# Gate and scale units of the adaLN in three slots of their own, and x loaded again behind gate B, in a two-layer trunk kernel

## The chip, the cores and the metric

The kernel runs on one core of one Trainium2 chip, in one launch. The metric is the device time of an execution in microseconds (us), median over runs. One further execution was taken by the hardware profiler; every row below is from it.

## What is computed

Two groups of tokens, 128 context tokens and 256 latent tokens, together 384, go through two layers of width 2048. Each layer modulates its input by shift and scale of an adaLN (a matrix-vector product of the conditioning with a weight of 2048 x 6144), multiplies it by one wide input projection, runs two branches, and adds a gated output projection to x:

```
shift, scale, gate = split(silu(cond) @ w_mod + b_mod, 3)
h    = rms_norm(x, g) * (1 + scale) + shift
proj = h @ w_in
# layer 0
a = ga * sigmoid(gb); a = depthwise_conv(a, 31 taps) + conv_b
a = silu(layer_norm(a, ln_g, ln_b)) * silu(gate_a)          # branch A
b = attention(rms_norm(q), rms_norm(k), v) * silu(gate_b)   # branch B
x = x + gate * (concat(a, b) @ w_out)
# layer 1: windowed attention with a sink, beside a short gated convolution; then a final rms_norm
```

## The kernel before, in words

Everything is in float32. A product of two matrices is made of three fp32r products: each operand is split into a high and a low part (`hi`, `lo`), and `hi*hi + hi*lo + lo*hi` is summed in PSUM. The activations stand transposed, 16 blocks k of 128 features by 384 tokens, as `hhi` and `hlo`. Weights come by SyncE's DMA queue (SP) in pieces of 512 KB into six buffers `raw` (L106); ScalarE (ACT) casts `whi` (L283), VectorE (DVE) takes the difference `wlo` (L284), and TensorE (PE) multiplies (L382). `proj_feat` makes 256 output features from two units; a unit is two such pieces and 48 products, the first over k 0 to 7, the second over k 8 to 15.

The stretch that matters is layer 0 behind its q, k and v. In order of the source: four blocks of `gb` and `ga` (16 units), four of gate A (8 units), four of gate B (8 units, the loop that the change touches), then `out_proj`, whose first unit needs k 0 to 7 of `mix`, that is branch A. Counting units from the first `gb` one, gate A begins at unit 16, gate B at 24, the output projection at 32. Beside the products run:

- the adaLN by matrix-vector products (`gemv_block`): a unit is 1 MB of `mod_w` and four products with 32 rows (L139). 28 of them wait in `gemv_q`: eight for the bias of q, 16 for layer 0's gate, four for a quarter of layer 1's scale. After each projection unit `pump` adds `bg["rate"]` to what is due and starts as many. Without slots of their own they load two pieces into the same `raw` buffers as the weights;
- the rest of layer 1's adaLN by rows (`mod_rows`): GpSimd's DMA queue (POOL, L91) brings rows of the transposed weight, DVE multiplies and sums them (L207). The first two of these sets work in `lent`, the room of x (16 blocks of 384 in the place `bigA`), cut into three pieces of 2048: two for rows, one as junk;
- attention: norms and rotary on DVE and ACT, then for each of six pairs of token block and head group scores (`s_ps`, L505), softmax (L510 to L521), transposes (`pT_ps`, L526) and the output (`o_ps`, L530);
- the convolution, 30 taps a block on DVE (L702), and behind it the layer norm: sum (`lsum`), mean by PE (L755), `apad - mean` (L761), sum of squares `lvar` (L768), by PE a sum over features (`rsl`, L240), a reciprocal root on DVE (L229 to L234), three diagonals `diag` (L255), and a PE product that spreads them over the partitions (`rbl`, L256). ACT copies that to `rb` (L262), DVE multiplies by it (L771), ACT applies silu (L772), DVE multiplies into `mix` (L793), and `mix` is split into `hhi` and `hlo` (L283, L284).

Each engine works its instructions off in one order, which a scheduler fixed when the program was built, from priorities and from its own idea of times; instructions under `later(LATER)` come behind others that are ready. An instruction that waits holds all behind it on its engine or queue.

Of the kernel before, what the change touches and what calls it, by code (L numbers as in the profile page):

```python
# [10 lines left out]
F32 = mybir.dt.float32  # L11
# [8 lines left out]
P = 128  # L20
D = 2048
KC = D // P
T = 384
# [14 lines left out]
LATER = 4000  # L38
# [3 lines left out]
FILL = 3  # L42
R0 = 1.7
SCALE_AT = (9, 11)
RA = 1.2
RB = 1.1
GRID_W = 64
GROUPS = ((0, 0, SEQ), (1, SEQ, T))

# [2 lines left out]
def trunk(ctx: ExitStack, tc: tile.TileContext, d: dict, o: dict):  # L52
    nc = tc.nc
    const = ctx.enter_context(tc.tile_pool(name="const", bufs=1))
    big = ctx.enter_context(tc.tile_pool(name="big", bufs=1))
# [7 lines left out]
    def aux(name):  # L63
        return ps_aux.tile([P, 512], F32, tag="aux", name=name)
# [13 lines left out]
    def vcol(name, i):  # L78
        return vec(name)[:, i:i + 1]
# [10 lines left out]
    def side_load(dst, src):  # L90
        ins = nc.gpsimd.dma_start(dst, src).ins  # L91
        if order["hold"] is not None:
            tc.add_manual_dep(ins, order["hold"].name, SYNC, reason="side loads wait")
# [20 lines left out]
    ring = {"slots": [], "n": 0}  # L114
# [7 lines left out]
    def gemv_block(w, f0, nf, stat, done):  # L122
        nk = 2048 // nf
        st = {}

        def unit(u):
            if u == 0:
                st["ps"] = ps_gv.tile([P, 512], F32, tag="gv", name="gv")
            ps = st["ps"]
            slot = ring_slot()  # L130
            if slot is not None:
                raws = [load_w(w, nk * u, nk, f0, nf, slot.rearrange("p (k f) -> p k f", f=nf))]
            else:
                raws = [load_w(w, nk * u + nk // 2 * i, nk // 2, f0, nf) for i in range(2)]
            for i in range(nk):
                g = i % 4
                k = nk * u + i
                raw = raws[i * len(raws) // nk]
                nc.tensor.matmul(ps[32 * g:32 * g + 32, :nf], lhsT=stat(k), rhs=raw[:, i % raw.shape[1], :],  # L139
                                 start=(k < 4), stop=(k >= KC - 4))  # L140
            if nk * (u + 1) == KC:
                gs = tmp.tile([P, 512], F32, tag="gs", name="gs", bufs=1)
                nc.scalar.copy(gs[:, :nf], ps[:, :nf])
                done(gs, ps)
        return [lambda u=u: unit(u) for u in range(KC // nk)]

    def mod_tile(layer, part):
        m = const.tile([P, KC, 2], F32, name=f"mod{layer}{part}")
        mods[layer, part] = m
        return m  # L150

    def mod_finish(layer, part, sl, parts):
        n = sl.stop - sl.start
        b = vec(f"mod_b{layer}")[:, 16 * part:16 * part + 16]
        gn = vec(f"norm_g{layer}")
        dst = mods[layer, part][:, sl, :]
        if parts is not None:
            nc.vector.tensor_reduce(dst, parts, AX.X, ALU.add)
        bb = b[:, sl].unsqueeze(2).broadcast_to([P, n, 2])
        nc.vector.tensor_tensor(dst, dst, bb, ALU.add)  # L160
        if part == 1:
            gg = gn[:, sl].unsqueeze(2).broadcast_to([P, n, 2])
            nc.vector.scalar_tensor_tensor(dst, dst, 1.0, gg, ALU.add, ALU.mult)

    def mod_part(layer, part, widths=(512, 512, 512, 512), f0=0):
        if (layer, part) not in mods:
            mod_tile(layer, part)

        def consume(f0, nf, gs, pc):
            n = nf // P  # L170
            for i in range(n):
                nc.tensor.transpose(pc[:, i * P:(i + 1) * P], gs[:, i * P:(i + 1) * P], ident)  # L172
            sl = slice(f0 // P, (f0 + nf) // P)
            mod_finish(layer, part, sl, pc[:, :nf].rearrange("p (k g r) -> p k r g", g=4, r=32)[:, :, 0:2, :])
        units = []
        for nf in widths:
            units += gemv_block(d[f"mod_w{layer}"][4 * part + f0 // 512], f0 % 512, nf, lambda k: cst[:, 2 * k:2 * k + 32],
                                lambda gs, ps, f0=f0, nf=nf: consume(f0, nf, gs, ps))
            f0 += nf
        return units  # L180
# [55 lines left out]
    def rstd_cols(parts, mean, name, behind=None):  # L236
        ps = aux(name)
        for n, av in enumerate(parts):
            for t in range(NT):
                order["sum"] = nc.tensor.matmul(ps[:, t:t + 1], lhsT=av[:, t * P:(t + 1) * P], rhs=ones,  # L240
                                                start=(n == 0 and t == 0),
                                                stop=(n == len(parts) - 1 and t == NT - 1)).ins
                if behind is not None:
                    tc.add_manual_dep(order["sum"], behind.name, NOSYNC, reason="not before its place")
        rs = const.tile([P, NT], F32, name=name)
        nc.vector.tensor_scalar(rs, ps[:, :NT], 1.0 / mean, EPS, ALU.mult, ALU.add)
        (pow_half if behind is None else rsqrt)(rs)
        return rs

    def by_token(rs, name):  # L250
        pb = aux(name)
        dgs = tmp.tile([P, T], F32, tag="wk", name="diag", bufs=4)
        for t in range(NT):
            dg = dgs[:, t * P:(t + 1) * P]
            nc.vector.tensor_scalar(dg, ident, rs[:, t:t + 1], None, ALU.mult)  # L255
            nc.tensor.matmul(pb[:, t * P:(t + 1) * P], lhsT=ones.broadcast_to([P, P]), rhs=dg, start=True, stop=True)  # L256
        return pb[:, :T]

    def rstd_rows(rs, name):
        pb = by_token(rs, name)  # L260
        rb = tmp.tile([P, T], F32, tag="rb", name="rb", bufs=1)
        nc.scalar.copy(rb, pb)  # L262
        return rb

    x = {"T": big.tile([P, KC, T], F32, tag="bigA", name="xT")}
# [47 lines left out]
    gemv_q = []  # L313
# [19 lines left out]
    @contextmanager  # L333
    def later(n):
        p = tc.cur_priority
        tc.cur_priority = p + n
        try:
            yield
        finally:
            tc.cur_priority = p + 1  # L340

    def drain(lst):
        while lst:
            lst.pop(0)()
# [49 lines left out]
    def proj_feat(w, evac, units=(0, 1), n=T):  # L394
        pp = pair()
        for u in units:
            feat_unit(pp, w, u, n, u == units[0], u == units[1])
        for j in range(2):
            evac(j, pp[j])
# [274 lines left out]
    def add_bias(b, gs, pb):  # L674
        for g, ts in ((0, (0,)), (1, (1, 2))):
            nc.tensor.matmul(pb, lhsT=selb[:, g, :], rhs=gs, start=True, stop=True)  # L676
            for t in ts:
                x = nat[t][:, 4 * b:4 * b + 4, :]
                nc.vector.tensor_tensor(x, x, pb.rearrange("p (h c) -> p h c", h=4), ALU.add)
    bias_q = [f for b in range(2) for f in  # L680
              gemv_block(d["wq0"][0], 512 * b, 512, lambda k: sst[:, k, :], lambda gs, ps, b=b: add_bias(b, gs, ps))]
# [4 lines left out]
    def attention0():  # L686
        ss = head_norms(nat, mix)
        for t in range(NT):
            qkv_tile(0, t, kT, v, nat, mix, 8, ss)
        for t in range(NT):  # L690
            for kv in range(NKV):
                attend(0, t, kv, kT, v, mix, 8)
# [14 lines left out]
        return [lambda j=j: tap(j) for j in range(CONF)] + [done]  # L707

    bg["rate"] = R0
    gemv_q.extend(bias_q + mod_part(0, 2) + mod_part(1, 1, (512,)))  # L710
    lent = big.tile([P, KC * T], F32, tag="bigA", name="lent")
    slots = [lent[:, i * D:(i + 1) * D] for i in range(3)]
    shifts = [mod_rows(1, 0, j, slots) for j in range(2)]
    x["T"] = big.tile([P, KC, T], F32, tag="bigA", name="xT2")
    with later(LATER):
        side_load(x["T"], d["xT"])
    for fb in range(4):
        sgs = []

# [15 lines left out]
        if fb == 1:  # L735
            attention0()
            bg["rate"] = RA
            room = mix[:, :8, :].rearrange("p c t -> p (c t)")
# [31 lines left out]
    def ln_out(c):  # L770
        ln["out"] = nc.vector.tensor_tensor(apad[:, c, :T], apad[:, c, :T], ln["r"], ALU.mult).ins  # L771
        nc.scalar.activation(apad[:, c, :T], apad[:, c, :T], AF.Silu, scale=vcol("ln_g0", c), bias=vcol("ln_b0", c))  # L772
    bg["rate"] = RB

# [5 lines left out]
    for fb in range(4):  # L780
        proj_feat(w0[12 + fb], evb(2 * fb))
        if fb == 0:
            ln_mean()
            for c in range(8):
                ln_center(c)
        if fb == 1:
            ln["r"] = rstd_rows(rstd_cols([ln["v"]], CW, "rsl", order["product"]), "rbl")
            for c in range(8):
                ln_out(c)
            shifts.append(mod_rows(1, 0, 3, vring, ln["out"]))  # L790
            scales = [mod_rows(1, 1, j, vring, ln["out"]) for j in (1, 2, 3)]
# [239 lines left out]
```

## Time and profile before

| | us |
|---|---|
| median of 3 runs | 1292.69 (1292.29 to 1292.76) |
| the profiled execution | 1290.78 |
| its span, first to last instruction | 1289.0 |
| PE, DVE, ACT, POOL busy | 1255.9, 884.3, 556.0, 96.1 |
| HBM read | 253 MB, 199 GB/s over the span |

The span is what lies between the first and the last instruction; 1.8 us of the profiled execution lie around it. PE's busy time counts pipelined products, so a full share does not say that it ran at its best.

### The profile page before, as it was taken

To read this page: it belongs to the slowest core of one execution; us is meant where nothing else is said; L and a number is where in the kernel's file an instruction comes from. 1 tells how busy PE (TensorE), PEld (TensorE's weight loads), DVE (VectorE), ACT (ScalarE), POOL (GpSimd) and SP (SyncE) were. 2 spreads that over 40 slices of the span, in tenths; PEclk is the share of its full clock that TensorE was granted. 3 is DMA by queue.
4 is the path that set the end of the run, shared out by engine and by line. 5 is a ranking of instruction groups with operands and counts; after the bars stand their busy time and mean duration, and the time that the engine had idled before them with its cause. 6 is when DMAs were issued, how large, how long until landed. Compare 5 with 4: busy or idle time off the path is not lost.

```text
span 1289.0 us, 17822 instructions
## 1 busy us (share of the span) xinstructions
PE 1255.9 (97%) x6856; PEld 1115.2 (87%) x6856; DVE 884.3 (69%) x1507; ACT 556.0 (43%) x983; POOL 96.1 (7%) x137
## 2 busy tenths in 40 slices
PE   6999999999999999999999999999999999999997
PEld 3566576778888899999999988899999999999997
DVE  2244688999899967999977933354544599994443
ACT  3345422554455655543464632354444432343322
POOL 0211200000000000111100000000000011101110
PEclk9999999999999999999999999999999999999999
DMA  9989887868665334577743443433333588843322
GB/s 364 395 308 357 348 312 302 327 234 286 219 201 177 129 99 148 188 265 259 245 155 111 130 131 119 135 114 115 98 99 98 175 268 270 265 148 124 124 66 98
DMA packets 70500, 257.97 MB, mean 200 GB/s; under 512 B 7376, under 2 KB 11728, under 8 KB 65424
## 3 DMA queue, kind: packets, MB, share of 16 engines
q1 hardware_dynamic: 57616, 203.51, 46.6%
q0 software_dynamic: 12656, 53.23, 11.8%
q8 instruction: 53, 0.87, 0.3%
q14 instruction: 31, 0.25, 0.1%
q10 hardware_dynamic: 144, 0.10, 0.0%
HBM read 253.15 MB, written 3.67 MB: 199 GB/s over the span
## 4 chain that ended last, share of the span: by engine, by line
PE 95%; DVE 2%; DMA 1%; ACT 1%; issue 1%; SPq 0%; DVEq 0%; ACTq 0%
PE pf L382 67%; PE pt L361 10%; PE q L612 6%; PE gv L139 5%; PE s_ps L505 2%; PE o_ps L530 2%; PE pT_ps L526 1%; DMA raw<-in_mod_w 1%; DMA ring<-in_mod_w 1%; PE y_ps L915 1%; PE gv L172 0%; DVE wlo L284 0%; PE qT_ps L491 0%; DVE hlo L284 0%; PE gv L676 0%
## 5 line engine op out<-in xcount | busy, mean ns | idle before, releaser
L382 PE MATMUL pf<-hhi,whi 128*128 128x384 f32 (+1 forms) x1664 | 568.8, 342 | 3.7 <-ACT whi L283 3.6
L382 PE MATMUL pf<-hlo,whi 128*128 128x384 f32 (+1 forms) x1664 | 569.9, 343 | 0.0
L382 PE MATMUL pf<-hhi,wlo 128*128 128x384 f32 (+1 forms) x1664 | 562.1, 343 | 1.5 <-DVE wlo L284 1.5
L284 DVE TENSOR_TENSOR wlo<-raw,whi 128x1024 fp32r<-128x1024 f32 x256 | 312.9, 1223 | 281.9 <-ACT whi L283 271.1
L283 ACT CAST whi<-raw 128x1024 fp32r<-128x1024 f32 x256 | 268.3, 1050 | 461.8 <-PE pf L382 237.6
L382 PEld LDWEIGHTS pf<-hhi,whi 128*128 128x128 f32 x1664 | 313.3, 188 | 23.5 <-issue 11.9
L382 PEld LDWEIGHTS pf<-hhi,wlo 128*128 128x128 f32 x1664 | 312.9, 188 | 16.2 <-issue 6.7
L382 PEld LDWEIGHTS pf<-hlo,whi 128*128 128x128 f32 x1664 | 313.8, 189 | 5.3 <-issue 3.0
L207 DVE CUSTOM_DVE_ANT_0 area<-area,crow 128x1024 f32<-128x1024 f32 x128 | 151.5, 1218 | 5.3 <-PE o_ps L530 4.4
L702 DVE SCALAR_TENSOR_TENSOR cv<-apad,cw,cv 128x399 f32<-128x399 f32 x240 | 138.0, 627 | 0.1
L91 POOL DMA_DIRECT2D area<-in_modT x64 | 34.0, 531 | 575.8 <-DVE sm L207 233.7
L361 PE MATMUL pt<-wlo,hhi 128*128 128x512 f32 x192 | 75.8, 395 | 0.0
L361 PE MATMUL pt<-whi,hhi 128*128 128x512 f32 x192 | 75.4, 396 | 0.0
L361 PE MATMUL pt<-whi,hlo 128*128 128x512 f32 x192 | 74.1, 395 | 0.0
L276 POOL TENSOR_TENSOR sacc<-sacc,sqf 128x384 f32<-128x384 f32 x28 | 33.5, 1195 | 176.7 <-ACT sqf L275 175.9
L361 PEld LDWEIGHTS pt<-whi,hhi 128*128 128x128 f32 x192 | 36.0, 188 | 11.0 <-ACT hhi L308 1.7
L612 PE MATMUL q<-whi,hhi 128*128 128x512 f32 x96 | 41.1, 428 | 4.4 <-ACT hhi L295 4.4
L361 PEld LDWEIGHTS pt<-whi,hlo 128*128 128x128 f32 x192 | 35.9, 188 | 10.0 <-DVE wlo L284 1.7
L361 PEld LDWEIGHTS pt<-wlo,hhi 128*128 128x128 f32 x192 | 36.1, 188 | 9.1 <-issue 0.8
L139 PE MATMUL gv<-ring,cst 128*32 128x512 f32 (+1 forms) x288 | 35.6, 582 | 8.5 <-DMA ring<-in_mod_w 7.6
L513 ACT ACTIVATE pr<-s_ps,nm 128x384 f32<-128x384 f32 (+1 forms) x48 | 24.4, 508 | 43.6 <-DVE nm L512 34.4
L612 PE MATMUL q<-wlo,hhi 128*128 128x512 f32 x96 | 40.5, 422 | 0.0
(186 smaller groups left out, 995.0 us busy)
## 6 DMA issues: line engine op xcount, KB each, us to landing
raw<-in_wf SPq DMA_DIRECT2D x144, 512.0 KB, 4.1
ring<-in_mod_w SPq DMA_DIRECT2D x32, 1024.0 KB, 7.5
area<-in_modT POOLq DMA_DIRECT2D x64, 512.0 KB, 5.2
raw<-in_w_out SPq DMA_DIRECT2D x64, 512.0 KB, 4.0
raw<-in_mod_w SPq DMA_DIRECT2D x40, 512.0 KB, 5.5
raw<-in_wq SPq DMA_DIRECT2D x32, 512.0 KB, 8.8
raw<-in_wt SPq DMA_DIRECT2D x24, 512.0 KB, 3.6
lent<-in_modT POOLq DMA_DIRECT2D x8, 1024.0 KB, 8.2
```

The lines of the kernel that those rows point to most:

```text
L91: ins = nc.gpsimd.dma_start(dst, src).ins
L139: nc.tensor.matmul(ps[32 * g:32 * g + 32, :nf], lhsT=stat(k), rhs=raw[:, i % raw.shape[1], :], start=(k < 4), stop=(k >= KC - 4))
L207: ins = nc.vector.tensor_tensor_reduce(out=raw if g else junk, in0=raw, in1=crow[:, g, h * n:(h + 1) * n], scale=1.0, scalar=0.0, op0=ALU. ...
L276: eng.tensor_tensor(av, av, s, ALU.add)
L283: nc.scalar.copy(dst_hi, src)
L284: order["split"] = nc.vector.tensor_tensor(dst_lo, src, dst_hi.bitcast(F32), ALU.subtract).ins
L361: nc.tensor.matmul(pp[t], lhsT=x[:, k, tt], rhs=y[:, i, :], start=(k == 0 and n == 0), stop=(k == KC - 1 and n == 2))
L382: ins = nc.tensor.matmul(pp[j][:, :n], lhsT=x[:, i, fj], rhs=y[:, k, :n], start=(begin and k % 8 == 0 and m == 0), stop=(end and k % 8 == ...
L505: nc.tensor.matmul(ps, lhsT=mix[:, h0 + h, t * P:(t + 1) * P], rhs=kT[:, kv, c0:c0 + nk * P], start=True, stop=True)
L530: nc.tensor.matmul(po, lhsT=v[:, slots[j], kv * HD:(kv + 1) * HD], rhs=pT[:, j, :], start=(j == 0), stop=(j == nk - 1))
L612: nc.tensor.matmul(pq[b][t], lhsT=x[:, k, tt], rhs=y[:, 0, 512 * b:512 * b + 512], start=(k == 0 and n == 0), stop=(k == KC - 1 and n == 2))
L702: nc.vector.scalar_tensor_tensor(st["o"], apad[:, c, j:j + CVW], cw[:, c, j:j + 1], st["o"], ALU.mult, ALU.add)
```

## The change

The units of layer 0's gate and of layer 1's scale no longer load into `raw`: from the first of them on, `ring["slots"]` names the three pieces of `lent`, so each unit is one load of 1 MB into one of these. The bias units of q stay in `raw`. The room therefore is not given back to x before gate B; behind gate B's second block (units 24 to 27) the queue of units is emptied, the slots are taken away, and the 3 MB of x are loaded on POOL's queue, not under `later` any more. The rates of `pump` after attention is written and after the convolution fall from 1.2 and 1.1 to 0.9 and 0.8, which spreads the 20 units.

```
-RA = 1.2
-RB = 1.1
+RA = 0.9
+RB = 0.8
...
     bg["rate"] = R0
-    gemv_q.extend(bias_q + mod_part(0, 2) + mod_part(1, 1, (512,)))
     lent = big.tile([P, KC * T], F32, tag="bigA", name="lent")
     slots = [lent[:, i * D:(i + 1) * D] for i in range(3)]
     shifts = [mod_rows(1, 0, j, slots) for j in range(2)]
-    x["T"] = big.tile([P, KC, T], F32, tag="bigA", name="xT2")
-    with later(LATER):
-        side_load(x["T"], d["xT"])
+
+    def own_slots():
+        ring["slots"] = slots
+    gates0 = mod_part(0, 2) + mod_part(1, 1, (512,))
+    gates0[0] = lambda unit=gates0[0]: (own_slots(), unit())
+    gemv_q.extend(bias_q + gates0)
...
         if fb == 1:
+            drain(gemv_q)
+            ring["slots"] = []
+            x["T"] = big.tile([P, KC, T], F32, tag="bigA", name="xT2")
+            side_load(x["T"], d["xT"])
             ln["r"] = rstd_rows(rstd_cols([ln["v"]], CW, "rsl", order["product"]), "rbl")
```

The first place at which the built order differs is SP's queue, around unit 6 (`in_wf` are weights, `in_mod_w` adaLN units). Before:

```order
L98 DMA raw<-in_wf 128x1024 x2
L98 DMA raw<-in_mod_w 128x1024 x4
L98 DMA raw<-in_wf 128x1024 x2
L98 DMA raw<-in_mod_w 128x1024 x2
L98 DMA raw<-in_wf 128x1024 x2
```

and after:

```order
L98 DMA raw<-in_wf 128x1024 x2
L98 DMA lent<-in_mod_w 128x2048 x2
L98 DMA raw<-in_wf 128x1024 x2
L98 DMA lent<-in_mod_w 128x2048
L98 DMA raw<-in_wf 128x1024 x2
```

The same bytes stand in the same places; half as many loads, and none of them takes a buffer of the weights.

The second is PE around `rbl`, the last product of the layer norm. Before, it stands inside the sixth unit of gate B (`pf1_4207` is a pair of that gate):

```order
L382 MATMUL pf1_4207<-hlo_94,whi_4300 128x384
L382 MATMUL pf1_4207<-hhi_93,wlo_4301 128x384
L256 MATMUL rbl_4080<-diag_4081,ones_83 128x128 x3
L382 MATMUL pf1_4207<-hhi_93,whi_4300 128x384
L382 MATMUL pf1_4207<-hlo_94,whi_4300 128x384
```

and after, where `pf1_4275` is the last pair of gate B and `pf0_4443` the first of the output projection:

```order
L382 MATMUL pf1_4275<-hlo_94,whi_4368 128x384
L382 MATMUL pf1_4275<-hhi_93,wlo_4369 128x384
L256 MATMUL rbl_4020<-diag_4021,ones_83 128x128 x3
L382 MATMUL pf0_4443<-hhi_93,whi_4447 128x384
L382 MATMUL pf1_4444<-hhi_93,whi_4447 128x384
L382 MATMUL pf0_4443<-hlo_94,whi_4447 128x384
```

Before, 102 products of gate B stand between `rbl` and the output projection; after, none. The mean of the layer norm (L755) moved the same way, from behind 26.98 units to behind 29.25, the sum for `rsl` from 28.94 to 31.10, and `rbl` from 29.88 to 32.00.

The third is DVE between the multiplication by `rb` and the first `hlo` of the output projection. Before, behind the eight L771:

```order
L207 ISA area,sm_4106<-area,crow 128x1024
L207 ISA sm_4106 128x1
L284 TENSOR_TENSOR wlo<-raw,whi 128x1024
L565 TENSOR_TENSOR mix_1217<-mix_1217,sg 128x384
L793 TENSOR_TENSOR mix_1217<-mix_1217,apad 128x384 x5
L207 ISA area,sm_4106<-area,crow 128x1024
L207 ISA sm_4106 128x1
L207 ISA area,sm_4106<-area,crow 128x1024
L207 ISA sm_4106 128x1
L793 TENSOR_TENSOR mix_1217<-mix_1217,apad 128x384 x3
L284 TENSOR_TENSOR wlo<-raw,whi 128x1024
L284 TENSOR_TENSOR hlo<-mix_1217,hhi 128x384 x3
```

and after, where the line numbers stand two and six higher (L773 is L771, L799 is L793):

```order
L773 TENSOR_TENSOR apad<-apad,rb 128x384 x8
L565 TENSOR_TENSOR mix_1217<-mix_1217,sg 128x384
L207 ISA area,sm_4046<-area,crow 128x1024
L207 ISA sm_4046 128x1
L284 TENSOR_TENSOR hlo<-mix_1217,hhi 128x384 x3
L799 TENSOR_TENSOR mix_1217<-mix_1217,apad 128x384 x7
L207 ISA area,sm_4046<-area,crow 128x1024
L207 ISA sm_4046 128x1
L207 ISA area,sm_4046<-area,crow 128x1024
L207 ISA sm_4046 128x1
L799 TENSOR_TENSOR mix_1217<-mix_1217,apad 128x384
L284 TENSOR_TENSOR hlo<-mix_1217,hhi 128x384 x8
```

The work is the same, but after, the splits of branch B's blocks (the three `hlo`, and the first of the eight) come ahead of branch A's, whose k 0 is the second of the eight. Ahead of L773 there now stand one `wlo` of unit 33 and three L565.

## Rows read from the trace of the kernel before

**Rows 1.** Span and mean granted clock of the core.
```profile
core 0: 1289.0 us, clock 0.995
```
**Rows 2.** The page's chain that ended last, shares of the span by engine.
```profile
PE 95%; DVE 2%; DMA 1%; ACT 1%; issue 1%; SPq 0%; DVEq 0%; ACTq 0%
```
**Rows 3.** Busy time by stretches; columns in the first line.
```profile
core 0: us, PE busy (x) PEld busy (x) DVE busy (x) ACT busy (x) POOL busy (x), PEclk, DMA share, GB/s
210.00:230.00 20.00, 18.81 (x99) 13.77 (x98) 18.93 (x27) 6.86 (x18) 0.53 (x1) 1.00 0.79 301
230.00:250.00 20.00, 16.98 (x91) 12.67 (x90) 19.83 (x38) 14.45 (x56) 0.00 (x0) 1.00 0.98 383
...
270.00:290.00 20.00, 17.82 (x96) 11.79 (x95) 17.37 (x27) 12.12 (x28) 1.38 (x3) 0.91 0.79 270
...
450.00:470.00 20.00, 20.00 (x107) 18.63 (x106) 17.62 (x30) 11.83 (x22) 0.00 (x0) 1.00 0.28 87
470.00:490.00 20.00, 20.00 (x110) 18.16 (x109) 10.80 (x18) 11.66 (x20) 1.57 (x3) 1.00 0.52 175
```
**Rows 4.** Chain that ended last, in order of time: start us, us, what.
```profile
236.89 5.81 DMA raw<-in_mod_w
...
272.37 3.77 DMA raw<-in_mod_w
...
508.77 9.49 PE pf L382 x54
...
518.29 1.09 DVE area L207
...
531.92 132.24 PE pf L382 x752
```
**Rows 5.** Waits of SP's queue, 225 to 285 us: total us, times, longest.
```profile
SPq L98 <- PE gv L139: 33.3, 10, 9.2
```
**Rows 6.** DVE in order of time, last set of rows in `lent`: start, us.
```profile
222.88 2.29 DVE L207 CUSTOM_DVE_ANT_0 lent<-lent,crow 128x2048 f32<-128x2048 f32 x1
```
**Rows 7.** Loads: size, median us to landing.
```profile
xT<-in_xT POOLq DMA_DIRECT2D x1, 3072.0 KB, 13.1
```
**Rows 8.** PE in order of time at `rbl` and in the output projection's first unit.
```profile
507.94 0.83 PE L256 MATMUL rbl<-diag,ones 128*128 128x128 f32 x6
...
531.92 0.45 PE L382 MATMUL pf<-hhi,wlo 128*128 128x384 f32 x1 [0.34 <-DVE wlo L284]
```
**Rows 9.** DVE in order of time, layer norm to first split.
```profile
500.15 0.16 DVE L246 TENSOR_SCALAR rsl<-rsl 128x3 f32<-128x3 f32 x1 [2.10 <-PE rsl L240]
...
503.81 0.68 DVE L255 TENSOR_SCALAR diag<-ident,rsl 128x128 f32<-128x128 f32 x3
...
509.32 3.84 DVE L771 TENSOR_TENSOR apad<-apad,rb 128x384 f32<-128x384 f32 x8 [1.15 <-ACT rb L262]
513.08 1.22 DVE L207 CUSTOM_DVE_ANT_0 area<-area,crow 128x1024 f32<-128x1024 f32 x1
...
515.83 2.42 DVE L793 TENSOR_TENSOR mix<-mix,apad 128x384 f32<-128x384 f32 x5
...
521.87 1.22 DVE L284 TENSOR_TENSOR wlo<-raw,whi 128x1024 fp32r<-128x1024 f32 x1
523.01 1.49 DVE L284 TENSOR_TENSOR hlo<-mix,hhi 128x384 fp32r<-128x384 f32 x3
```
**Rows 10.** ACT in order of time, the same stretch.
```profile
508.81 0.48 ACT L262 COPY rb<-rbl 128x384 f32<-128x384 f32 x1 [1.22 <-PE rbl L256]
...
511.02 4.89 ACT L772 ACTIVATE apad<-apad,vecs 128x384 f32<-128x384 f32 x8
515.82 1.04 ACT L283 CAST whi<-raw 128x1024 fp32r<-128x1024 f32 x1
```
**Rows 11.** Busy time behind two waits of PE; columns as in Rows 3.
```profile
46.20:53.58 7.38, 7.38 (x28) 5.63 (x32) 3.29 (x9) 2.81 (x8) 0.00 (x0) 0.77 1.01 415
276.20:280.00 3.80, 3.80 (x10) 1.46 (x12) 3.80 (x7) 1.97 (x4) 0.00 (x0) 0.55 1.01 372
```

## The prediction, made before the changed kernel ran

> **What bounds the kernel now.** I read the core's line first: one core, a span of 1289.0 us, clock 0.995 [rows 1], so at most half a per cent is lost to the clock over the whole. Then the chain of waits: 95% of what ended last is PE [rows 2]. A change therefore gains only where PE waits or runs at the lower clock, and it loses wherever it makes PE wait. Then busy time by stretches of 20 us, to find where PE is not full: the stretch 210:230 has 18.81 us of products, 230:250 has 16.98, 270:290 has 17.82, and by 450 every stretch is full [rows 3]. Last the chain in order of time, for what PE waits for in these stretches: 5.81 us and 3.77 us of a load of `mod_w` into `raw` [rows 4]. So the adaLN units hold PE up there. Two things make them late. Their loads share the six `raw` buffers and SP's queue with the weights; that queue waited 33.3 us in 225 to 285 for the products of units (`gv`), which free those buffers [rows 5]. And the 3 MB of x, which needed 13.1 us to land [rows 7], came into the same stretch, where the DMA engines were busy 0.98 of the time at 383 GB/s [rows 3]: nothing can be loaded earlier there without something else coming later.
>
> **What the change takes away.** The units load into three slots that no weight uses, and x leaves this stretch. PE's idle time is 20 − 16.98 = 3.0 us in 230:250 and 20 − 17.82 = 2.2 in 270:290 [rows 3]. In 270:290 the granted clock was also 0.91 [rows 3]. The chip has two levels, 1.2 and 2.4 GHz; 0.91 of 20 us is 1.8 us of full speed lost, and the row that holds the low part alone, 3.80 us at 0.55, shows 0.45 × 3.8 = 1.7 [rows 11]. Together 3.0 + 2.2 + 1.7 = **6.9 us**. The most that could go is 9.0: the 1.2 us of 210:230 and some 0.9 of small waits besides. The least I take is 4: the slots are pieces of `lent`, whose last reduction on DVE runs until 222.88 + 2.29 = 225.2 [rows 6], and a slot is loaded again only when the unit before in it is multiplied, so that a slot's load can hold SP's queue, and the weights behind it, as a buffer of `raw` did.
>
> [...]
>
> **What it moves: x.** The reload goes behind unit 27, to 460 to 470. There the DMA engines are 0.28 busy [rows 3]. It takes 13.1 us if it lands as before [rows 7]; x is read first where the output projection is evacuated, tens of us later. Behind it on POOL's queue stand only rows for `area`, which wait for attention's buffers in any case. I cost it at 0; without that cover the rows would come 13 us later, and DVE, which has them to reduce, is busy for only 10.80 of 20 us at 470:490 [rows 3].
>
> **What it moves: the rates.** The 20 units stay, and so does their work on PE. The rates 0.9 and 0.8 end them some four units of projection later, so that the queue is nearly empty when the new drain comes: 0.
>
> **What it moves without saying so.** This is the large term. In the built order the convolution's end, the layer norm and `rbl` stand some 2.1 units later against the products. A unit is 48 products of 132.24 / 752 = 0.176 us [rows 4], 8.4 us, so 18 us later. Before, the products of gate B between `rbl` and the output projection number 102, or 18 us, and they cover this chain: `rbl` at 507.94 [rows 8], `rb` on ACT at 508.81 [rows 10], eight L771 from 509.32, the areas' L207, eight L793, the split of the first block from 523.01 [rows 9]. That `hlo` (three take 1.49, so one 0.5) is ready at 523.5, 15.6 us behind `rbl`, and PE is still at gate B; all the output projection waits for is 0.34 us, later [rows 8]. After, no product stands between. PE has nothing to do from `rbl` until the chain is through.
>
> I add up the chain from T, the last product of gate B, along DVE's new order, each from its row [rows 9, 10]:
> - ACT's `whi` of the next weight, whose buffer frees at T: 1.0; DVE's `wlo`: 1.15 (1.22, less the overlap with its neighbour); three L565 at 0.47: 1.4. T + 3.6; the `rb` is made beside that.
> - eight L773 (was L771): 3.8 [rows 9]. T + 7.4.
> - an L565 0.5, an area L207 1.15, three `hlo` of branch B 1.4. T + 10.4.
> - seven L799 (was L793; five took 2.42): 3.3. T + 13.7. ACT's eight silu, 4.89 [rows 10], run alongside.
> - two L207 2.3, the eighth L799 0.5. T + 16.5.
> - one `hlo` of branch B, then that of k 0, which PE wants: 0.9. T + 17.4.
>
> PE does `rbl` (0.83 for six [rows 8], some 0.67 of its own) and two products with `hhi` (0.35) in that time, so its wait is 17.4 − 1.0 = **16.4 us**. The lower end is the 15.6 of before less two `wlo` between (2.3): 13.3. The upper is 18.5, if `diag`, which is to be ready about at T, is a `wlo` and an ACT step late.
>
> Behind a wait this long the clock has to be counted. Two rows show what stood behind waits before: 7.38 us at 0.77, a loss of 0.23 × 7.38 = 1.7, and 3.80 at 0.55, also 1.7 [rows 11]. I take 2.5 for a longer wait, between one such loss and two (1.7 to 3.4). The 0.34 us wait of before goes [rows 8].
>
> **Sum.** −6.9 + 16.4 + 2.5 − 0.3 = **+11.7 us**. The profiled execution took 1290.78 us, 1.8 of it around its span, so 1302.5 on its own footing. The median of the runs, 1292.69, is 1.9 above it: **1304.4 us**. With the ends: −9.0 + 13.3 + 1.7 − 0.3 = +5.7, 1298.4; −4.0 + 18.5 + 3.4 − 0.3 = +17.6, 1310.3.
>
> **Rivals.**
> *The layer norm does not show; only the waits go.* On the chip DVE may run well ahead of PE: at 470:490 it is idle for 9.2 of 20 us [rows 3], and it waits 2.10 us for the sum behind `rsl` [rows 9]; if its mean, squares and roots were through long before T, the chain would shrink. The gain of 6.9 then stays: 1290.78 − 6.9 + 1.9 = 1285.8. This decides from the point at which PE's wait with its clock comes under 7 us. Against it: the order has `rbl` behind the last product of gate B, on PE's queue, which runs in order, so the eight multiplications by `rb`, at 3.84, those by `apad` and the split cannot begin sooner, however early DVE is. These alone are 3.8 + 3.9 + 0.5 = 8.2. 12%.
> The Trainium skill's "Perfetto Trace Analysis", section "Optimization Strategy", would favour this rival: the same gap repeated on the engine that should be full can mean too few buffers for the next tile. The waits for `raw` agree with it; of what the longer hold on these buffers does later it says nothing.
>
> *About equal.* A wait of 9 us with little clock behind it, against a gain of 9.0. Within 0.2% (2.6 us, which is about what a measurement of this kernel can tell from no change). It needs both at their edge: 8%.
>
> *The slots hold SP's queue.* The change doesn't do what it says: with three slots, a load waits for the unit three back, the weights stand behind it in the same queue, and PE waits at each for a landing, as it did for 5.81 and 3.77 [rows 4]. Then nothing is gained and the chain costs as above: +16.4 + 2.5 − 0.3 = 18.6, less at most a few: 1309 to 1312. For it: DVE keeps `lent` until 225.2 [rows 6], and the first units are due about there. Against it: half as many loads are issued, and the DMA engines have 13 us less to carry in that stretch. 8%.
>
> **How the numbers follow.** The forecast, slower by 5.7 to 17.6 us, has 72%, its dearer rival 8%, the equal case 8%, the faster one 12%. So slower by over 0.2% has 0.80, within it 0.08, faster 0.12. The range for 8 in 10 is that of the forecast, widened a little downwards for a chain that is partly hidden and up to the dear rival's middle: 1297 to 1311.
>
> **What would show it.** In the profile of the changed kernel: stretches 230 to 290 with PE at 19.5 or more of 20 and the clock at 1.00 (the gain); no wait of SP's queue for `gv` above a few us; x landing within some 13 us near 465 while PE stays full; behind `rbl` a wait of PE of 13 to 18 us, ended by DVE's `hlo`, with the clock below 1.00 in the stretch behind it. The forecast is wrong if `rbl` runs some 10 us before gate B's last product, or if PE's wait there ends below 7 us; and if the waits for `raw` return as waits for slots.

## The result, and the profile after

The changed kernel took 1300.5 us (median of 6 runs, 1300.38 to 1301.07), the kernel before, run beside it, 1292.49 (6 runs, 1287.83 to 1293.07). The ratio is 1.0071, with a 95% interval of 1.0061 to 1.0081: slower by 0.6 to 0.8%. The forecast was 1304.4 us and a range of 1297 to 1311.

The profiled executions are 1290.78 us before and 1300.42 after, 9.6 us apart. The core's line after, which answers [rows 1]:

```profile
core 0: 1298.6 us, clock 0.990
```

Busy time by stretches of the changed kernel, which answers [rows 3] (same columns):

```profile
230.00:250.00 20.00, 20.00 (x118) 16.75 (x118) 18.46 (x34) 13.70 (x54) 0.00 (x0) 1.00 0.75 285
...
270.00:290.00 20.00, 20.00 (x129) 18.14 (x129) 19.83 (x33) 14.44 (x31) 1.32 (x3) 1.00 1.00 399
...
510.00:530.00 20.00, 12.03 (x73) 11.66 (x71) 15.80 (x37) 13.60 (x24) 0.00 (x0) 0.87 0.34 106
530.00:550.00 20.00, 12.39 (x59) 11.89 (x60) 20.00 (x40) 6.55 (x12) 5.08 (x5) 0.71 0.28 87
...
650.00:690.00 40.00, 40.00 (x231) 40.00 (x230) 29.86 (x52) 28.79 (x63) 2.87 (x4) 1.00 0.47 149
```

The reader is to see three things. Where PE was not full before, at 230:250 and 270:290, it now has 20.00 of 20 at a clock of 1.00. Where it was full (39.7 of 40 at 510 to 550), it now has 24.4 of 40, and the clock is lower. And a stretch that the prediction did not name, 650:690, is full too; before it was not:

```profile
650.00:690.00 40.00, 38.09 (x217) 37.36 (x216) 26.07 (x46) 24.98 (x54) 2.17 (x3) 1.00 0.36 112
```

What PE does at the place of the loss, in order of time, which answers [rows 8]:

```profile
521.10 0.93 PE L256 MATMUL rbl<-diag,ones 128*128 128x128 f32 x6
532.65 1.01 PE L382 MATMUL pf<-hhi,whi 128*128 128x384 f32 x2 [10.62 <-ACT hhi L283]
538.61 0.69 PE L382 MATMUL pf<-hlo,whi 128*128 128x384 f32 x1 [4.96 <-DVE hlo L284]
```

`rbl` follows the last product of gate B at once, and behind it PE waits 10.62 us for `hhi` and, two products later, 4.96 us for `hlo`: 15.58 us. DVE in the same stretch, which answers [rows 9]:

```profile
522.18 1.23 DVE L284 TENSOR_TENSOR wlo<-raw,whi 128x1024 fp32r<-128x1024 f32 x1 [0.75 <-ACT whi L283]
523.32 1.49 DVE L565 TENSOR_TENSOR mix<-mix,sg 128x384 f32<-128x384 f32 x3
524.73 3.83 DVE L773 TENSOR_TENSOR apad<-apad,rb 128x384 f32<-128x384 f32 x8
...
528.95 1.22 DVE L207 CUSTOM_DVE_ANT_0 area<-area,crow 128x1024 f32<-128x1024 f32 x1
...
530.09 1.49 DVE L284 TENSOR_TENSOR hlo<-mix,hhi 128x384 fp32r<-128x384 f32 x3
531.50 3.36 DVE L799 TENSOR_TENSOR mix<-mix,apad 128x384 f32<-128x384 f32 x7
...
537.07 0.55 DVE L799 TENSOR_TENSOR mix<-mix,apad 128x384 f32<-128x384 f32 x1
537.54 3.83 DVE L284 TENSOR_TENSOR hlo<-mix,hhi 128x384 fp32r<-128x384 f32 x8
```

DVE has no gap from 522.18 on: PE waits for a queue of work, not for one slow operation. The clock between the two waits and behind the second, in shorter stretches:

```profile
531.00:535.00 4.00, 1.01 (x2) 0.50 (x2) 4.00 (x10) 2.92 (x7) 0.00 (x0) 0.50 0.00 0
...
537.00:539.00 2.00, 0.39 (x1) 0.39 (x2) 2.00 (x7) 0.51 (x1) 1.32 (x1) 0.50 0.65 211
539.00:541.00 2.00, 2.00 (x7) 2.00 (x7) 2.00 (x6) 0.00 (x0) 1.65 (x1) 0.50 0.13 51
541.00:543.00 2.00, 2.00 (x11) 2.00 (x11) 2.00 (x4) 0.00 (x0) 0.19 (x1) 0.81 0.00 0
543.00:545.00 2.00, 2.00 (x13) 2.00 (x12) 2.00 (x4) 0.94 (x1) 0.34 (x1) 1.00 0.43 94
```

The clock was already at the lower level, 1.2 GHz (0.50), when the first wait ended, and PE works at it behind the second, from 538.6 to about 541.8. That loses 0.2 + 1.0 + 0.4 = 1.6 us.

To see where kernels part, the same product is looked up in each: the first of a unit of 48. The table gives its start less its start before, both counted from the first product of unit 5 (225.4 us before), which lies ahead of anything that the change touches. Unit 31 is the last of gate B, unit 34 stands behind the start of the output projection, and unit 52 is in layer 1.

| kernel | unit 31 | unit 34 | unit 52 | median, us |
|---|---|---|---|---|
| changed | -5.8 | +12.9 | +10.2 | 1300.5 |
| e2 slots, old rates | -7.7 | +8.0 | +5.2 | 1296.73 |
| e3 `mean` pinned | -2.7 | +3.5 | +0.7 | 1290.65 |
| e5 x held, no slots | -4.4 | +12.2 | +9.4 | 1300.87 |
| e6 areas later | -5.8 | +11.2 | +8.5 | 1298.95 |
| e7 pinned, areas later | -2.7 | -3.3 | -1.2 | 1289.03 |
| e8 rates alone | +3.2 | +4.3 | +1.5 | 1292.46 |
| e9 fillers | -5.8 | +14.0 | +11.2 | 1300.66 |
| e10 pinned, areas behind block 7 | -2.7 | -2.7 | -3.6 | 1286.83 |
| e11 as e10, `mean` earlier | +2.6 | +2.6 | +1.7 | 1291.37 |
| e12 as e10, x held, no slots | -2.8 | -2.9 | -3.7 | 1287.24 |

The differences are those of single profiled executions; in these the kernel before itself moves by some 2 us either way (see the last section).

### The profile page after: what moved, and what is told of

Same layout as the page of the kernel before. It is cut to its first block, busy times and chain, and to the rows that moved or that the text cites. A ratio compares the mean times of both kernels' runs of the same rounds, so it can differ in the third digit from the quotient of the medians.

```text
span 1298.6 us, 17795 instructions
## 1 busy us (share of the span) xinstructions
PE 1257.6 (97%) x6856; PEld 1116.1 (86%) x6856; DVE 884.9 (68%) x1507; ACT 564.6 (43%) x989; POOL 96.3 (7%) x137
## 4 chain that ended last, share of the span: by engine, by line
PE 96%; DVE 2%; DMA 1%; ACT 0%; issue 0%; SPq 0%; DVEq 0%; ACTq 0%
PE pf L382 68%; PE pt L361 10%; PE q L612 6%; PE gv L139 5%; PE s_ps L505 2%; PE o_ps L530 2%; PE pT_ps L526 1%; DMA ring<-in_mod_w 1%; PE y_ps L921 1%; PE gv L172 0%; PE qT_ps L491 0%; PE gv L676 0%; DVE mix L799 0%; DVE apad L773 0%; DVE area L207 0%
## 5 line engine op out<-in xcount | busy, mean ns | idle before, releaser
L382 PEld LDWEIGHTS pf<-hhi,wlo 128*128 128x128 f32 x1664 | 313.7, 189 | 12.2 <-issue 4.7
L207 DVE CUSTOM_DVE_ANT_0 area<-area,crow 128x1024 f32<-128x1024 f32 x128 | 151.3, 1218 | 4.9 <-PE o_ps L530 4.4
L513 ACT ACTIVATE pr<-s_ps,nm 128x384 f32<-128x384 f32 (+1 forms) x48 | 24.4, 509 | 44.2 <-DVE nm L512 34.4
```

The lines of the kernel that those rows point to most:

```text
L207: ins = nc.vector.tensor_tensor_reduce(out=raw if g else junk, in0=raw, in1=crow[:, g, h * n:(h + 1) * n], scale=1.0, scalar=0.0, op0=ALU. ...
L382: ins = nc.tensor.matmul(pp[j][:, :n], lhsT=x[:, i, fj], rhs=y[:, k, :n], start=(begin and k % 8 == 0 and m == 0), stop=(end and k % 8 == ...
```

## The experiments

Theory O says that the loss is the place of the layer norm against the products: `rbl` has no products behind it that cover its chain. Its rivals are that the rates, the late load of x, the slots or the lower clock cost the time. Theories A and B are about the gain: the 3 MB of x crowded the loads, or the shared `raw` buffers held them up.

**e1, the reload written behind gate B.**

```diff
-    x["T"] = big.tile([P, KC, T], F32, tag="bigA", name="xT2")
-    with later(LATER):
-        side_load(x["T"], d["xT"])
...
         if fb == 1:
+            drain(gemv_q)
+            x["T"] = big.tile([P, KC, T], F32, tag="bigA", name="xT2")
+            side_load(x["T"], d["xT"])
```

> The kernel before, with only the reload of x put behind gate B's second block; the adaLN units still load into `raw`, the rates stay 1.2 and 1.1. Layer norm and `rbl` stand in the built order where they stood before (`rbl` behind 29.88 units). Theory A (x's 3 MB crowded the loads): PE's waits at 238 and 273 us go, as they did in the changed kernel, and no new wait comes: 1292.5 - 5 = 1287.5, 1285 to 1289. Theory B (the shared buffers and SP's queue made them): the waits stay within 2 us of the 5.2 of before: 1290 to 1293. Both: no wait of 10 us or more at the output projection.

Measured: 1291.46 us, ratio 1.0002 (0.9989 to 1.0015). The edit did not do what it says. The loads of 215 to 290 us and a stretch of e1:

```profile
xT<-in_xT POOLq DMA_DIRECT2D x1, 3072.0 KB, 13.5
```

```profile
270.00:290.00 20.00, 17.88 (x106) 11.93 (x105) 15.99 (x24) 11.98 (x26) 1.06 (x2) 1.00 0.85 304
```

x was still loaded in that stretch: where the line stands in the program holds nothing on POOL's queue, and without slots in `lent` the room was free. So this run says nothing on A and B.

**e5, x really held.** As e1, and the load waits for the last product of unit 27:

```diff
+            order["hold"] = order["product"]
             side_load(x["T"], d["xT"])
+            order["hold"] = None
```

> The kernel before, with the reload of x made to wait for the last product of gate B's second block (in the run that only wrote it there, the load still started at 225 us, since nothing on POOL's queue held it). The adaLN units load into `raw` as before. In the built order this alone puts `rbl` behind 31.96 units (29.88 before). Theory A (x's 3 MB crowds the loads): PE's idle time in 230 to 290 us falls from 5.2 us to under 2. Theory B (the shared buffers make the waits): it stays at 4 us or more. Theory O (the place of the layer norm costs the time): in both cases PE waits 13 to 16 us behind `rbl`, so by A + O the time is some 1291 - 5 + 17 - 2 = 1301 and by B + O some 1305; if the place does not matter, 1286 to 1292.

Measured: 1300.87 us, ratio 1.006 (1.0043 to 1.0077).

```profile
230.00:250.00 20.00, 19.23 (x112) 14.76 (x110) 17.93 (x35) 14.29 (x55) 0.00 (x0) 1.00 0.61 210
...
270.00:290.00 20.00, 20.00 (x130) 18.01 (x127) 18.56 (x32) 15.03 (x38) 0.55 (x1) 1.00 0.77 275
```

```profile
521.71 0.83 PE L256 MATMUL rbl<-diag,ones 128*128 128x128 f32 x6
531.22 1.01 PE L382 MATMUL pf<-hhi,whi 128*128 128x384 f32 x2 [8.33 <-ACT hhi L283]
537.19 0.69 PE L382 MATMUL pf<-hlo,whi 128*128 128x384 f32 x1 [4.96 <-DVE hlo L284]
```

With no slot at all, 0.8 us of the 5.2 us of idle time are left: for PE's waits A holds and B falls. And the wait behind `rbl` is there, 8.33 + 4.96 = 13.3 us, though neither slots nor rates were touched. Holding x back is enough for both halves of the result.

**e2, the changed kernel with the old rates, and e8, the rates alone.**

```diff
-RA = 0.9
-RB = 0.8
+RA = 1.2
+RB = 1.1
```

> The changed kernel with the rates at 1.2 and 1.1 again. `rbl` stands behind 31.81 units in the built order (32.00 in the changed kernel, 29.88 before): 9 products are left to cover the chain. Theory O (the place of the layer norm costs the time, and the slots moved it): PE waits 15.6 - 1.6 = 14 us, some 1299, 1297 to 1301. Rival (the slower rates moved it, or the later units cost it): back to 1286 to 1289.

Measured: 1296.73 us, ratio 1.0052 (1.0031 to 1.0073), a little below the range; PE's waits behind `rbl` are 7.8 and 5.0 us, 12.8 against 14 expected. e8 makes the opposite edit in the kernel before:

> The kernel before with the rates 0.9 and 0.8 and nothing else. `rbl` stands behind 30.00 units (29.88 before). Theory O (the slots and x's absence moved the layer norm, the rates hardly): no wait over 2 us at the output projection, time within 1.5 us of before, 1289.5 to 1292.5. Rival (the slower rates alone bring a part of the loss): slower by 3 us or more.

Measured: 1292.46 us, ratio 1.0008 (0.9997 to 1.002), and PE is full from 490 to 530. The rates alone make no loss that the times can tell, but in the trace PE is 3.2 us late at unit 31. On top of the late x they may add some 3.8 us by the medians (1300.5 less 1296.73), though the intervals of the two ratios overlap.

**e3, the mean pinned.** One order for PE's queue, no wait on the chip:

```diff
+MEAN_AT = 28
...
                         ins = nc.tensor.matmul(pp[j][:, :n], lhsT=x[:, i, fj], rhs=y[:, k, :n],
...
+                        if order["unit"] == MEAN_AT * 48:
+                            tc.add_manual_dep(ins, order["mean"].name, NOSYNC, reason="behind the mean")
+                        order["unit"] += 1
```

> The changed kernel with one order added: the first product of unit 28 stands behind the layer norm's `mean` product. In the built order `mean` then stands behind 28.0 units (29.25 in the changed kernel), `rbl` behind 30.56 (32.00): 69 products or 12.1 us cover the chain. The sum for the mean was ready at 477.8 us in the changed kernel, and unit 28 began at 482, so nothing should wait there. Theory O: the wait of 15.6 falls to about 3.5 and half of the lost clock comes back: 1300.5 - 12.1 - 0.8 = 1287.6, 1285 to 1290. Rival (the convolution is really later on the chip, since the units run earlier): PE waits the same 10 us or more at `mean` instead, 1297 to 1301.

Measured: 1290.65 us, ratio 1.0008 (0.9996 to 1.002), 9.9 us below the changed kernel by the medians and some 8 us by the ratios, and just above the range. PE in order of time:

```profile
487.07 0.81 PE L761 MATMUL mean<-lsum,ones 128*128 128x384 f32 x2
...
509.93 0.83 PE L257 MATMUL rbl<-diag,ones 128*128 128x128 f32 x6
...
525.27 0.44 PE L383 MATMUL pf<-hlo,whi 128*128 128x384 f32 x1 [2.05 <-DVE hlo L285]
...
531.98 0.45 PE L383 MATMUL pf<-hlo,whi 128*128 128x384 f32 x1 [0.65 <-DVE hlo L285]
534.99 0.44 PE L383 MATMUL pf<-hlo,whi 128*128 128x384 f32 x1 [1.68 <-DVE hlo L285]
```

`mean` runs without a wait and the wait behind `rbl` falls from 15.6 to 4.4 us. So the late place was not forced by the convolution. In the changed kernel the last sum for `mean` was done on DVE at 477.8, and PE took it up only at 496.63:

```profile
477.29 0.55 DVE L755 TENSOR_TENSOR lsum<-lsum,apad 128x384 f32<-128x384 f32 x1
```

The kernel was 3 us dearer than expected. The two later waits (0.65 and 1.68) were not foreseen: branch B's last blocks are split late, behind reductions into `area`. And unit 31 is only 2.7 us ahead, not 5.8: with `mean` pinned, PE also waits 0.98 us in attention and does `rsl` and `rbl` before it (1.2 us).

**e4, branch B first in the output projection,** on top of e3:

```diff
-    out_proj(0, d["w_out0"], mix, (0, 1), each, 2, ahead)
+    out_proj(0, d["w_out0"], mix, (1, 0), each, 2, ahead)
```

> As the one with `mean` pinned, and the output projection's units take branch B first, so that 48 products that need no layer norm stand ahead of its first use. Theory O: the rest of the wait (3.5 us) goes too, 1284 to 1287. Rival: branch B's own last blocks, multiplied by the gate behind gate B's last product and split behind the chain on DVE, are late in their turn, and PE waits 3 us or more for them: 1287 to 1291.

In this kernel the last two pairs multiply blocks of layer 1's input in place of branch A's, since `ahead` overwrites blocks 0 to 7; their sizes are the same. Measured: 1297.07 us, ratio 1.0051 (1.0031 to 1.0071). The rival was right, and too mild:

```profile
525.61 0.44 PE L383 MATMUL pf<-hlo,whi 128*128 128x384 f32 x1 [1.12 <-DVE hlo L285]
...
533.25 0.44 PE L383 MATMUL pf<-hlo,whi 128*128 128x384 f32 x1 [2.85 <-DVE hlo L285]
541.10 0.69 PE L383 MATMUL pf<-hlo,whi 128*128 128x384 f32 x1 [5.48 <-DVE hlo L285]
```

PE now asks first for the blocks that DVE makes last. The order on PE and the order on DVE have to be changed together.

**e6, the reductions into `area` later,** in the changed kernel. `mod_rows` for the last four sets is called behind the splits of the output projection, and its reductions are ordered behind the last of these:

```diff
-            shifts.append(mod_rows(1, 0, 3, vring, ln["out"]))
-            scales = [mod_rows(1, 1, j, vring, ln["out"]) for j in (1, 2, 3)]
...
+    def area_sets():
+        shifts.append(mod_rows(1, 0, 3, vring, order["split"]))
+        scales.extend(mod_rows(1, 1, j, vring, order["split"]) for j in (1, 2, 3))
```

> The changed kernel, with the reductions into `area` put behind the last split of the output projection on DVE. `rbl` stays behind 32.00 units. Of the chain behind `rbl` three L207 of 1.14 us leave, the three splits of branch B stay. Theory O (PE waits for exactly this chain on DVE): the wait falls by 3.4 us, from 15.6 to 12.2, and the time to 1297 (1295.5 to 1298.5). Rival (ACT's `hhi` or another engine sets it): no change, 1300. Rival (the reductions, 3 to 9 us later on a DVE that is 96% busy, end later than they are needed at features 9 and 11): what is gained comes back as waits around 620 to 690 us, 1300.

Measured: 1298.95 us, ratio 1.005 (1.0031 to 1.0069). PE's waits behind `rbl`:

```profile
530.41 1.01 PE L382 MATMUL pf<-hhi,whi 128*128 128x384 f32 x2 [9.47 <-ACT hhi L283]
535.23 0.69 PE L382 MATMUL pf<-hlo,whi 128*128 128x384 f32 x1 [3.82 <-DVE hlo L284]
```

13.3 us against 15.6: two L207 (2.3 us) left the chain, and the third stands again ahead of the `hlo` that PE wants, since branch B's last block, behind which the reductions are ordered, is split before branch A's. The median fell by 1.6 us, to 0.45 us above the range, and the intervals of the two ratios overlap; it is the shorter wait that shows that PE waits for this chain.

**e7, both,** e3 and e6 together.

> The changed kernel with `mean` pinned and the reductions into `area` behind the last split. By theory O the chain behind `rbl` (509.9 us there) is through at 521, before gate B ends at 523, so PE waits for nothing at the output projection: 1290.65 less the waits of 4.4 and the lost clock of 1.8 is 1284.4, 1283 to 1286.5. Rival (DVE is the bound of the output projection once the reductions are late): waits of 2 to 9 us come back before 690, 1287 to 1293.

Measured: 1289.03 us, ratio 0.9977 (0.9968 to 0.9986): faster than both kernels, but 2.5 us above the range.

```profile
510.00:530.00 20.00, 20.00 (x118) 20.00 (x118) 18.72 (x35) 17.29 (x31) 3.44 (x2) 1.00 0.40 127
...
650.00:690.00 40.00, 37.08 (x204) 36.43 (x204) 29.29 (x51) 23.27 (x50) 3.23 (x5) 0.96 0.47 145
```

No wait is left at the output projection. The rival was right as well, with 2.9 us of wait and a lower clock in 650:690. PE waits there for ACT, 1.00 us for a `whi` and 1.93 us for an `hhi` of layer 1's input; the last reduction starts at 669.5 us, against 658.7 in e3.

**e10, the reductions behind block 7's split instead of block 15's,** otherwise e7.

> As the one with `mean` pinned and the reductions into `area` late, but behind the split of block 7 instead of block 15, so that the first of them run some 6 us earlier. That one lost 2.9 us in waits at 667 and 670 and about 1.5 in clock behind them. If the late reductions made these: 1289.0 - 4 = 1285, 1284 to 1287. Rival (they come from elsewhere, the order of ACT there): 1288 to 1290.

Measured: 1286.83 us, ratio 0.9963 (0.995 to 0.9976), the fastest of all.

```profile
530.00:550.00 20.00, 19.69 (x113) 19.37 (x112) 18.78 (x31) 6.23 (x11) 2.12 (x4) 1.00 0.65 211
...
650.00:690.00 40.00, 38.76 (x222) 38.10 (x221) 30.16 (x52) 24.68 (x52) 3.23 (x5) 1.00 0.50 160
```

Idle time in 650:690 falls from 2.9 to 1.2 us and the clock is 1.00. What went is the wait for `hhi`, so the place of the reductions had made it; the wait for `whi`, 0.95 us, stays. It is not their end that counts, for the last one starts at 670.2 us, as late as in e7.

**e11, `mean` still earlier:** e10 with `MEAN_AT = 26.5`, which puts it behind 27.25 units in the built order.

> As e10, with `mean` behind 27.25 units and `rbl` behind 30.06 in the built order, nearly as before (26.98, 29.88). The sum for `mean` was ready at 477.8 us, and 27.25 units are done at 474 to 476 us, so PE may wait 2 to 4 us at `mean`; nothing is gained behind `rbl`, where e7 had no wait left: 1286 to 1290. If DVE's convolution moves with it, no wait, 1284 to 1287.

Measured: 1291.37 us, ratio 0.9997 (0.9988 to 1.0007), 4.5 us above e10 and above both ranges.

```profile
470.00:490.00 20.00, 16.90 (x65) 11.47 (x64) 8.08 (x18) 10.16 (x25) 1.05 (x2) 0.83 0.13 35
```

PE idles for 3.1 us and then runs at a lower clock. The wait is not at `mean` itself but ahead of it, at attention's transposes of `pr`, the result of its softmax (2.5 and 0.5 us), which the scheduler put ahead of `mean`, behind the same 27.25 units. Earlier is not better once the work ahead is not ready.

**e12, e10 without the slots:** the kernel before with x held as in e5, `mean` pinned and the reductions behind block 7.

> The kernel before (units in `raw`, old rates) with the reload of x held back as in e5, `mean` pinned and the reductions into `area` late as in e10; so e10 without the slots. In e5 PE's idle time in 230 to 290 us was 0.8 us against 0 with the slots, and up to unit 31 it had gained 4.4 us against 6.2 in the changed kernel. If x's absence is what gains and the slots add the small rest: 1286.8 + 1 to 2 = 1288, 1286.5 to 1289.5. Rival (the slots are needed, the waits for `raw` come back as wider ones once the planner packs them otherwise): 1290 or more. Rival (the slots add nothing): 1286 to 1287.

Measured: 1287.24 us, ratio 0.9973 (0.9963 to 0.9984). The interval overlaps that of e10. This does not show that the slots are worth nothing: e12 has the old rates and e10 the slower ones, so a gain of the slots and a loss by the rates can cancel.

**e9, fillers.** 55 products of no use between `rbl` and the output projection of the changed kernel:

```diff
+    pd = aux("fill")
+    for i in range(FILLERS):
+        ins = nc.tensor.matmul(pd[:, :T], lhsT=hhi[:, 15, :P], rhs=hhi[:, 15, :T], start=True, stop=True).ins
+        tc.add_manual_dep(ins, order["rbl"].name, NOSYNC, reason="behind the layer norm")
```

> The changed kernel with 55 products of no use (block 15 of the activations by itself, into a PSUM tile that nothing reads) between `rbl` and the output projection: 55 x 0.176 = 9.7 us of the 10.6 us in which PE waits there for `hhi`. DVE's and ACT's order is the same. If the lower clock comes from PE's long wait, the granted clock stays at 1.00 until the wait of 5 us for `hlo`, and the time falls by what the clock cost behind the wait, 1.4 us by the rows of the changed kernel (2 us at 0.50 and 2 us at 0.81), to 1299, 1298 to 1300. Rival (the second wait, 5 us, drops the clock by itself): no change, 1300 to 1301. Rival (the end is not set by this chain): 1305 or more.

Measured: 1300.66 us, ratio 1.0075 (1.0058 to 1.0091): the first rival. 9.7 us more work on PE cost nothing, which is theory O once more. Nor did it save the clock:

```profile
533.00:535.00 2.00, 0.00 (x0) 0.00 (x0) 2.00 (x5) 1.40 (x3) 0.00 (x0) 1.00 0.00 0
535.00:537.00 2.00, 0.00 (x0) 0.00 (x0) 2.00 (x4) 0.35 (x1) 0.86 (x2) 0.78 0.20 31
537.00:539.00 2.00, 1.40 (x4) 1.40 (x5) 2.00 (x6) 0.17 (x1) 2.00 (x1) 0.50 0.63 231
539.00:541.00 2.00, 2.00 (x8) 2.00 (x8) 2.00 (x4) 0.00 (x0) 0.64 (x1) 0.50 0.00 0
541.00:543.00 2.00, 2.00 (x8) 2.00 (x7) 2.00 (x5) 0.00 (x0) 0.53 (x1) 0.51 0.00 0
```

The wait that was left, 5.25 us, brought the lower level by itself, and for longer than in the changed kernel.

## Why the prediction was right, and where its terms were off

**The sign and the mechanism were right.** What it read out of the built order, 102 products behind `rbl` before and none after, is what the trace shows, and e3, e5 and e9 show that this makes the loss.

**The wait: 16.4 forecast, 15.6 measured.** The addition held step by step. With T at 521.0 (`rbl` starts at 521.1), the forecast put the end of the three L565 at 524.6, of L773 at 528.4, of branch B's splits at 531.4, of seven L799 at 534.7, of the eighth at 537.5 and the first `hlo` of branch A at 538.4. Measured, by the start of what follows on DVE, were 524.7, 528.5, 531.5, 534.8, 537.5 and, from PE, 538.6. The 0.8 us between the sums is that PE's own two products took 1.0 us at the low clock and not 0.35, that `rbl` took 0.93 and not 0.67, and that it followed a little behind T.

**The clock: 2.5 forecast, 1.6 measured,** below its lower end of 1.7. A longer wait did not cost more clock than the short ones of [rows 11].

**The gain: 6.9 forecast, some 4.6 measured.** In 230:250 and 270:290 all of it came. One reading was loose: 5.81 and 3.77 us are the lengths of two loads on the chain, not what PE waited. Its own waits of before, 5.0 of the 5.2 us, are these:

```profile
238.83 1.05 PE L139 MATMUL gv<-raw,cst 128*32 128x512 f32 x4 [1.12 <-DMA raw<-in_mod_w]
241.57 0.44 PE L382 MATMUL pf<-hhi,whi 128*128 128x384 f32 x1 [1.69 <-ACT whi L283]
...
276.19 1.80 PE L139 MATMUL gv<-raw,cst 128*32 128x512 f32 x4 [2.18 <-DMA raw<-in_mod_w]
```

The sum took PE's idle time and not these lengths, so it does not suffer. But unit 31 is only 5.8 us earlier, and 1.2 of these are `rsl` and `rbl`, which before had been done by then (six products each, 0.59 and 0.58 us from start to start). The 2.3 us that are missing went to the slower rates, which the prediction had put at 0. With the old rates and the same slots (e2) unit 31 is 7.7 us earlier, of which 0.6 is `rbl`: 7.1, the whole gain. The 160 products of the gate and scale units tell it, in the changed kernel first and in e2 second (count, PE's busy time, mean ns of one):

```profile
L139 PE MATMUL gv<-lent,cst 128*32 128x512 f32 x160 | 26.9, 603 | 0.0
L139 PE MATMUL gv<-lent,cst 128*32 128x512 f32 x160 | 24.6, 602 | 0.0
```

One of them takes as long in both, but at the slower rates they stand in 23 groups between other products and not in 20, and overlap less. e8 shows the same without slots: 29.0 us against 25.7 before. The lower end of 4 covered it.

**The cause of the gain: x for the waits, the slots open.** The prediction named two things that made the units late, the shared buffers and x. In e5 x alone takes 4.4 of the 5.2 us of waits away. The slots may be worth something all the same: with the old rates and a late x, unit 31 is 7.7 us earlier with slots (e2) and 4.4 without (e5), and the medians are 1296.73 and 1300.87. 0.8 us of that are waits, and 2.1 are again the units' products, 26.7 us in e5. The intervals of the two ratios overlap, so this is not settled. One of the prediction's signs failed: it wanted no long wait of SP's queue for `gv`, and the changed kernel has longer ones than [rows 5]:

```profile
SPq L98 <- PE gv L139: 41.8, 6, 12.9
SPq L98 <- DVE sm L207: 9.5, 1, 9.5
```

The 9.5 us behind `lent`'s last reduction are the dear rival's mechanism. It took place and cost PE nothing: PE has no wait from 225 to 290 us, so what it needed had landed before. A waiting queue is no loss until its consumer waits.

**x at 0 and the drain at 0** held: x took 12.6 us to land, in a stretch where PE is full.

**The rates at 0** did not hold. Beside the 2.3 us above they leave PE 2.8 us more of wait (15.6 against 12.8 in e2). The prediction counted their 20 units, but not that they shift the chain by another 0.2 units and take the last 9 products behind `rbl`, 1.6 us; the rest is DVE's order, whose way from `rbl` to `hlo` is 16.2 us in e2 and 17.5 here. The forecast of the wait was read from the built order, so it had this part in it. At unit 52 the changed kernel is 10.2 us late and e2 5.2: about half of the loss in these executions goes with the rates.

**A term that was missing: 1.9 us in 650:690,** as a gain. Before, PE waits there for the start of layer 1 (`whi` of ACT, 1.58 us at 673). After, PE comes 12 us later and ACT's `whi` only 8 us later (680.37 against 672.17), so it is done in time. The prediction had no term for it; a wait that is put into the bounding engine takes from later waits what its partners do meanwhile. e7 and e10 show the reverse: with the early wait gone, 2.9 and 1.2 us come back there.

The terms as measured, the gain less what the rates took of it: -4.6 + 15.6 + 1.6 - 0.3 - 1.9 = +10.4, against 9.6 between the profiled executions and 10.2 by the table at unit 52. The forecast of +11.7 came close partly by luck: the early gain was 2.3 us too large, and the wait, the clock and the missing gain at layer 1 erred the other way by 3.6.

**The rivals.** The faster one failed at the point that the prediction gave: PE's queue runs in order, and `rbl` stood behind the last product, however early DVE was (its sum for `mean` was ready 19 us ahead of PE). Too few buffers, the reading that the Trainium skill's "Perfetto Trace Analysis", section "Optimization Strategy", offers for repeated gaps, is not what these waits were: e5 left the six buffers alone and 4.4 of the 5.2 us went.

Why does the scheduler put the layer norm later when x goes? e5 shows that x's place alone does it, and e3 that the chip doesn't need it. That the scheduler, seeing fewer waits of PE, lays more products ahead of DVE's convolution fits this, but was only argued.

## What to carry to other kernels

When a change takes waits off the bounding engine, look in the built order for what that engine's products covered elsewhere: work on the other engines keeps its length, and the cover moves. A product that stands late in an in-order queue may be early in its data; compare when its input was written with when it ran, and pin it where the input is ready, not earlier (e3 and e10 against e11). And move a load by something that its queue has to wait for: its place in the program may hold nothing (e1 against e5). Where a change has several parts, take each back by itself: the slower rates cost here what a sum had put at nothing (e2).

## What the runs showed of the hardware

The clock's fall behind a short wait differs from one execution to the next. The profiled execution of before has 17.82 us of products in 270:290 at a clock of 0.91 [rows 3]; e1's has 17.88 there at 1.00, and e8's shows the fall at the other wait:

```profile
230.00:250.00 20.00, 17.18 (x84) 11.94 (x83) 19.83 (x37) 13.90 (x52) 0.00 (x0) 0.91 0.97 373
```

The runs of the kernel before agree over their whole length: about 1288 us at a mean clock of 0.998, 1289.4 to 1291.6 at 0.995, 1292.0 to 1294.1 at 0.993. One execution's clock loss behind a wait of 2 to 3 us is thus a chance and no fixed term of a sum: it fell behind one of 1.93 us in e7 (one of 1.00 us stands 3 us ahead of it) and not behind one of 2.85 in e4. Behind waits of 5 us that began at the full clock (5.25 in e9, 5.48 in e4) it fell both times; in the changed kernel it had fallen in the wait of 10.62 us and was still low at the one of 4.96. The Trainium skill's "TensorE: Matmul & The Clock Gate", section "Why this matters for your kernels", advises against idle gaps above a certain length between bursts of products, since one such puts the array back to its lower level; the runs agree for the waits of 5 us and more, and show the fall behind shorter ones too, in some executions.
